# First norm tile by tile, gate projection of block 3 ahead of block 2's, and the GLU operand split between the last projection units

## The chip, the cores and the metric

The kernel runs on one core of a Trainium2 chip. The core has TensorE (PE, matmul), VectorE (DVE), ScalarE (ACT), GpSimd (POOL) and SyncE (SP, which here only issues transfers), each with its own in-order instruction stream, and 16 DMA engines. The metric is device microseconds of one execution, lower is better. The kernel before takes 2582.24 us, the median of 3 runs (2581.13 to 2583.32).

## The reference

Two residual layers with sandwich RMSNorm, for a prompt of 2048 tokens and 32 sample tokens that share the weights (model width 1024, float32):

```python
# layer 0, chunked gMLP
hn = rmsnorm(x, norm_pre[0])
u, v, z = split(hn @ w_in_a, 3)              # each 2048 wide
v = layernorm(v)
s = lower_triangular_mix_of_128(v) + b_s     # 8 groups
x = x + rmsnorm((u * s * silu(z)) @ w_out_a, norm_post[0])
# layer 1, S5
xb, z = split(rmsnorm(x, norm_pre[1]) @ w_in_b, 2)   # each 1024 wide
h = complex_diagonal_scan(xb)                # 64 groups of 16 channels, 64 states
y = gelu(Re(C h) + d_skip * xb)
y = (y @ w_glu1 + b_glu1) * sigmoid(y @ w_glu2 + b_glu2)
x = x + rmsnorm((y * silu(z)) @ w_out_b, norm_post[1])
```

It returns x for both groups, the normalised v rows of the sample and the last states.

## The kernel before

Every large product is float32 split in two float32r parts, high and low, and takes three matmuls (high by high, high by low, low by high; `mm3`, L62). The split of an operand is a cast on ScalarE (L69) and a subtraction on VectorE (L70). Weights come in pieces of 128x1024 (512 KB) through a staging tile `wst` and are split into `whi` and `wlo` (`weight`, L72).

The 2048 prompt tokens are four blocks of 512; the 32 sample tokens ride with block 3, so a product over block 3 that has tokens as its free dimension takes two banks of 256 and 288 columns, where another block takes one of 512 (`cols`, L317).

*Start.* `layer_a` (L478) loads four tiles x of 128 tokens, and for each: two squares on ScalarE (L135), the mean and a root by Newton steps on VectorE (L104 to L109, L136, L137), the product with the norm's gain (L140), eight PE transposes (L146) and the split into `hn`. Ahead of it 40 warm-up matmuls on a tile of ones run on PE (L193). Then `v_phase` (L250) multiplies `hn` with `wv`, weight piece by weight piece, over four banks (one for each tile of 128 tokens).

*End of layer B.* `layer_b` (L757) makes the inputs of the state space, the states `S` at every eighth position (a scan on VectorE), and then two things side by side: the last 16 pieces of the gate projection (`z_phase`, L846, one piece of 128 channels over one block each, first the 8 of block 2 and then the 8 of block 3) and 16 projection units (`s5_out`, L920). A unit loads T, Xo and Co (and, every second unit, Go) by SP, copies states into H on ScalarE, runs four matmuls with T and Xo and four with Co and H, takes the gelu on ScalarE into `Y` (L957), and stores `Y` to the DRAM tensor `yd` from GpSimd (L960). Each z piece is copied on ScalarE and stored from ScalarE's queue (L860; for block 3 the sample's columns too, L859).

*Start of layer C.* `layer_c` (L997) reads `yd` back, piece k of 128 channels at a time, into staging tiles `yst` (`load_y`, L1018) and splits it into `y`. One piece needs two units: k = 0 the units 0 and 2, k = 4 the units 1 and 3, and so on; the order of the pieces is `KO = (0, 4, 1, 5, 2, 6, 3, 7)`. `glu` (L1033) then multiplies `y` with two weights for each of 8 channel pieces.

The order in which instructions stand on each engine is set when the program is built, by a scheduler that takes the emitted order, the dependencies and its own model of times. On the chip each engine runs its stream in that order, and an instruction waits on semaphores for what it reads and for the buffer that it writes. Pools of buffers are stacked: a pool that opens after another has closed lies over its memory, and its first tile waits for the last use of the old one. So `y` (pool `yq`, opened after `hb3` has closed) lies over the normalised block 3.

Of the kernel before, what the change touches and what calls it, by code (L numbers as in the profile page):

```python
# [8 lines left out]
F32 = mybir.dt.float32  # L9
F32R = mybir.dt.float32r  # L10
# [9 lines left out]
TB = 512  # L20
NS = 32
TX = TB + NS
AL = 512
TXP = 640
# [6 lines left out]
KO = (0, 4, 1, 5, 2, 6, 3, 7)  # L31
# [3 lines left out]
class Trunk:  # L35
# [151 lines left out]
    def consts_a(self, c, tmp):  # L187
        nc, I = self.nc, self.I
        self.one = c.tile([128, 128], F32, name="one")
        nc.vector.memset(self.one, 1.0)  # L190

        b = self.aux()
        for i in range(40):  # L193
            self.mm(b[:, 0:128], self.one, self.one, True, True)
        self.gpre = self.load_gpre(c, 0)
        self.consts()
# [53 lines left out]
    def v_phase(self, b, hn, hook=None):  # L250
        nc, I = self.nc, self.I
# [7 lines left out]
        for n in range(4):  # L259
            bk = [self.bank() for _ in range(4 + smp)]  # L260
            for kp in range(4):
                w = self.weight(I["wv"][n, kp], (2, 512))
                for kk in range(2):
                    k = kp * 2 + kk
                    wk = (w[0][:, kk], w[1][:, kk])
                    f, l = k == 0, k == 7
                    for i in range(4):
                        c = slice(i * 128, i * 128 + 128)
                        self.mm3(bk[i], (hn[:, 0, k, c], hn[:, 1, k, c]), wk, f, l)
                    if smp:  # L270
                        self.mm_sample(bk[4][:64, :], self.stk[:, k], wk, f, l)
            vq = self.vg.tile([128, 4, 512], F32, tag="vg", name="vq", align_bytes=AL)
            for i in range(4):
                nc.scalar.copy(vq[:, i], bk[i])
                nc.vector.bn_stats(st[:, i, n], bk[i])
            self.vq.append(vq)
            if hook:
                hook(n)
            if smp:
                vs = self.vs[:NS, n * 512:n * 512 + 512]  # L280
                self.fold_sample(vs, bk[4])
                nc.vector.bn_stats(sts[:, n], vs)
# [195 lines left out]
    def layer_a(self):  # L478
        I = self.I
        with ExitStack() as s:  # L480
# [5 lines left out]
            xs0 = self.prep_load([I["xp"][0, 0]], 128)  # L486
            self.consts_a(ca, self.xp)
            hn, jobs = self.prep_jobs(0, I["xp"][0], I["xs"], self.gpre, self.hnp, "hn", None, 1)
            xs = [xs0] + [f() for f, _ in jobs[1:]]
            for (_, f), x in zip(jobs, xs):  # L490
                f(x)
            self.pin = True
            fin = None

# [11 lines left out]
            for b in range(NB):  # L506
# [6 lines left out]
                if b + 1 < NB:  # L513
# [3 lines left out]
                    hn, jobs = self.prep_jobs(b + 1, I["xp"][b + 1], I["xs"], self.gpre, self.hnp, "hn", self.stk)  # L517
                else:
                    g1 = self.load_gpre(ca, 1)
                    hn, jobs = self.prep_jobs(0, self.x1c(0), None, g1, self.hnp, "hn")  # L520
# [236 lines left out]
    def layer_b(self, s0):  # L757
        with ExitStack() as sr:
            zp = s0.enter_context(self.pool("zp", 2))
            with ExitStack() as s1:  # L760
                hb3 = s1.enter_context(self.pool("hb3"))
                with ExitStack() as s2:
                    hb2 = s2.enter_context(self.pool("hb2"))
                    with ExitStack() as s3:
                        hb1 = s3.enter_context(self.pool("hb1"))
                        with ExitStack() as s4:
# [5 lines left out]
                            jobs = []  # L772
# [13 lines left out]
                            for _ in steps:  # L786
                                pass
                        S = self.hnp.tile([128, 32, 2, CW + 1], F32, tag="hn", name="S",
                                          align_bytes=AL).rearrange("p g r c -> p r g c")
# [15 lines left out]
                    opa = sr.enter_context(self.pool("opa", 2, side="right"))  # L805
                    fp = sr.enter_context(self.pool("fp", side="right"))
                    out = self.s5_out(fp, opa, opb, S)
                    n = 0
                    for i in range(16):
                        if i == 8:  # L810
                            s2.close()
                        self.z_phase(zp, [2 + i // 8], [i % 8])
                        while n < 16 and n * 13 <= i * 15:
                            next(out)
                            n += 1
            self.yq = s0.enter_context(self.pool("yq"))
            self.yp = s0.enter_context(self.pool("yp", 2))
            self.y0 = self.load_y(0)

    def relay(self, dst, o, c0, n):  # L820

# [98 lines left out]
    def s5_out(self, fp, opa, opb, S):  # L920
        nc, I = self.nc, self.I
# [3 lines left out]
        for u in range(16):  # L925
            gl, gh, gu = (u // 2) * 4, u % 2, ((u // 2) % 2) * 4
            fb = u // 4 + 4 * gh
            g0 = fb * 8 + gu
            T = opa.tile([128, 4, 128], F32, tag="T", name="T", bufs=4)
            nc.sync.dma_start(T, self.td[fb][:, gu:gu + 4])  # L930
            X = opa.tile([128, 4, 2, CW], F32, tag="X", name="Xo", bufs=4)
            self.load_x(X, fb, gu, 4)
# [13 lines left out]
            p = slice(gh * 64, gh * 64 + 64)  # L946
# [50 lines left out]
    def layer_c(self):  # L997
        nc, I = self.nc, self.I
        with ExitStack() as s:
# [12 lines left out]
            for q in range(4):  # L1012
# [2 lines left out]
                    y = self.load_y(q + 1)  # L1015
                self.out_b(q, m, stk)

    def load_y(self, q):  # L1018
        nc = self.nc
        y = self.yq.tile([128, 2, 8, TXP], F32R, tag="y", name="y", align_bytes=AL)  # L1020
        for k in KO:
            t = self.yp.tile([128, TX], F32, tag="y", name="yst")
            n = TB
            nc.sync.dma_start(t[:, :TB].rearrange("p (j c) -> p j c", j=4),
                              self.yd[k].rearrange("j k g c -> (k g) j c")[:, 4 * q:4 * q + 4, :])
            if q == 3:
                n = TX
                nc.sync.dma_start(t[:, TB:].rearrange("p (j c) -> p j c", j=4),
                                  self.ysd[k].rearrange("j k g c -> (k g) j c"))
            self.split(y[:, 0, k, :n], y[:, 1, k, :n], t[:, :n])  # L1030
        return y

    def glu(self, q, y):  # L1033
# [212 lines left out]
```

## Time and profile before

| what | value |
|---|---|
| median of 3 runs | 2582.24 us (2581.13 to 2583.32) |
| the profiled execution | 2583.09 us |
| its span in the profile | 2581.3 us |
| PE busy | 2554.0 us, 99% |
| VectorE, ScalarE, GpSimd busy | 58%, 36%, 17% |
| mean rate of the DMA engines | 145 GB/s |

The span is the time from the first to the last instruction of the profiled execution; what is between it and that execution's own time, 1.8 us, lies around it. PE is the engine to read: its busy time is modelled from the issue of matmuls, so small gaps in it are best seen in the list of PE's waits and in the timeline, where a row has its start, its length, its engine, line and operands, and in brackets the idle time before it with what ended it. A view by windows gives the busy time of each engine in a stretch, the clock granted to PE (1.00 is full speed) and the share of the DMA engines.

### The profile page before, as it was taken

How to read it: one execution, taken by the hardware profiler on the slowest of the kernel's cores; microseconds unless marked ns; L12 is line 12 of the kernel's file. 1: busy time of each engine (PE TensorE's matmuls, PEld its weight loads, DVE VectorE, ACT ScalarE, POOL GpSimd, SP SyncE). 2: the span in 40 equal slices, each digit the busy share in tenths (PEclk: the TensorE clock that was granted, in tenths of full speed). 3: DMA queues.
4: the chain of work that ended last, by engine and by line, in shares of the span. 5: the costliest groups of instructions: out<-in, count | busy, mean ns of one | idle time of the engine just before them, and what ended most of it. 6: DMA issues, size and time to landing. Idle time of an engine off the chain costs nothing.

```text
span 2581.3 us, 34682 instructions
## 1 busy us (share of the span) xinstructions
PE 2554.0 (99%) x13163; PEld 2183.2 (85%) x13163; DVE 1501.7 (58%) x2809; ACT 926.2 (36%) x1520; POOL 429.5 (17%) x624
## 2 busy tenths in 40 slices
PE   9999999999999999999999999999999999999998
PEld 8888888788888888887999877889888888888896
DVE  5955657745655755744633547417897346464645
ACT  3322443323443222532222344325556433434331
POOL 0345100455100000000100120000023212121220
PEclk9999999999999999999999999999999999999999
DMA  5333424343534454343322346537699545454533
GB/s 168 100 127 112 135 95 151 116 122 115 153 116 130 163 162 155 109 138 93 105 78 82 107 128 191 145 110 212 215 321 303 186 132 183 138 183 144 163 123 102
DMA packets 220631, 375.04 MB, mean 145 GB/s; under 512 B 59520, under 2 KB 135808, under 8 KB 220464
## 3 DMA queue, kind: packets, MB, share of 16 engines
q1 hardware_dynamic: 165728, 308.09, 37.6%
q0 software_dynamic: 13600, 39.90, 4.9%
q10 hardware_dynamic: 41136, 24.84, 3.4%
q8 instruction: 103, 1.69, 0.3%
q14 instruction: 64, 0.52, 0.1%
HBM read 311.64 MB, written 61.11 MB: 144 GB/s over the span
## 4 chain that ended last, share of the span: by engine, by line
PE 89%; DVE 5%; DMA 3%; issue 1%; ACT 1%; SPq 0%; POOL 0%; DVEq 0%; ACTq 0%; POOLq 0%
PE mm L60 85%; PE aux L60 3%; DMA x<-in_xp_dram 1%; DVE wlo L70 1%; PE aux L146 1%; DMA x<-x1d 1%; ACT junk L135 0%; DMA T<-td 0%; DMA Xo<-xd 0%; DVE nt L107 0%; DMA wst<-in_wib_dram 0%; ACT whi L69 0%; DVE o L175 0%; DVE nt L108 0%; DMA Xi<-xd 0%
## 5 line engine op out<-in xcount | busy, mean ns | idle before, releaser
L60 PE MATMUL mm<-hn,whi 128*128 128x512 f32 (+2 forms) x3840 | 1011.1, 351 | 0.0
L70 DVE TENSOR_TENSOR wlo<-wst,whi 128x1024 fp32r<-128x1024 f32 x400 | 516.3, 1292 | 536.0 <-ACT whi L69 520.6
L60 PEld LDWEIGHTS mm<-hn,whi 128*128 128x128 f32 x3840 | 671.6, 189 | 88.0 <-DVE a L345 0.2
L69 ACT CAST whi<-wst 128x1024 fp32r<-128x1024 f32 x400 | 419.7, 1050 | 860.4 <-PE mm L60 758.6
L60 PE MATMUL mm<-hn,wlo 128*128 128x512 f32 (+2 forms) x1920 | 673.2, 351 | 2.9 <-DVE wlo L70 2.9
L60 PEld LDWEIGHTS mm<-hn,wlo 128*128 128x128 f32 x1920 | 361.7, 188 | 48.4 <-DVE wlo L70 3.3
L60 PE MATMUL mm<-y,whi 128*128 128x512 f32 (+2 forms) x1280 | 333.8, 350 | 3.1 <-ACT y L69 2.9
L60 PE MATMUL mm<-whi,gs 128*128 128x512 f32 x1024 | 328.4, 393 | 2.2 <-ACT a L344 1.4
L60 PE MATMUL mm<-whi,hn 128*128 128x512 f32 x1024 | 324.4, 392 | 0.6 <-ACT hn L69 0.6
L60 PEld LDWEIGHTS mm<-y,whi 128*128 128x128 f32 x1280 | 224.7, 188 | 34.8 <-ACT y L69 3.6
L60 PEld LDWEIGHTS mm<-whi,gs 128*128 128x128 f32 x1024 | 191.6, 188 | 44.9 <-ACT a L344 1.7
L60 PEld LDWEIGHTS mm<-whi,hn 128*128 128x128 f32 x1024 | 192.6, 189 | 43.5 <-ACT hn L69 0.9
L60 PE MATMUL mm<-y,wlo 128*128 128x512 f32 (+2 forms) x640 | 223.1, 349 | 0.0
L60 PE MATMUL mm<-wlo,hn 128*128 128x512 f32 x512 | 200.2, 391 | 0.1
L60 PE MATMUL mm<-wlo,gs 128*128 128x512 f32 x512 | 199.8, 390 | 0.0
L70 DVE TENSOR_TENSOR gs<-gq,gs 128x512 fp32r<-128x512 f32 (+1 forms) x128 | 91.1, 714 | 133.7 <-ACT gs L69 133.4
L60 PE MATMUL mm<-whi,m 128*128 128x512 f32 x512 | 159.8, 389 | 0.0
L69 ACT CAST gs<-gq 128x512 fp32r<-128x512 f32 (+1 forms) x128 | 80.5, 629 | 190.3 <-PE mm L60 175.4
L60 PEld LDWEIGHTS mm<-y,wlo 128*128 128x128 f32 x640 | 120.8, 189 | 15.1
L60 PEld LDWEIGHTS mm<-wlo,hn 128*128 128x128 f32 x512 | 96.4, 188 | 21.5 <-DVE wlo L70 0.5
L358 DVE SCALAR_TENSOR_TENSOR gq<-mm,lng,Rp 128x512 f32<-128x512 f32 x64 | 47.9, 748 | 114.5 <-PE mm L60 114.5
L60 PEld LDWEIGHTS mm<-whi,m 128*128 128x128 f32 x512 | 96.1, 188 | 20.7
(287 smaller groups left out, 2624.0 us busy)
## 6 DMA issues: line engine op xcount, KB each, us to landing
wst<-in_wuz_dram SPq DMA_DIRECT2D x128, 512.0 KB
wst<-in_wv_dram SPq DMA_DIRECT2D x64, 512.0 KB
wst<-in_woa_dram SPq DMA_DIRECT2D x64, 512.0 KB
wst<-in_wg_dram SPq DMA_DIRECT2D x64, 512.0 KB
wst<-in_wib_dram SPq DMA_DIRECT2D x48, 512.0 KB
wst<-in_wob_dram SPq DMA_DIRECT2D x32, 512.0 KB
Xi<-xd SPq DMA_DIRECT2D x32, 272.0 KB
Xo<-xd SPq DMA_DIRECT2D x32, 272.0 KB
```

Source lines behind the costliest of these rows:

```text
L60: self.nc.tensor.matmul(out, lhsT, rhs, start=start, stop=stop)
L69: self.nc.scalar.copy(hi, src)
L70: return (e or self.nc.vector).tensor_tensor(lo, src, hi.bitcast(F32), SUB)
L146: nc.tensor.transpose(b[:, k * 128:k * 128 + P], x[:, o:o + 128], self.ident[:P, :P])
L358: nc.vector.scalar_tensor_tensor(g3, s3, self.lng[:, db:db + 1], R, MUL, ADD)
```

## The change

1. The warm-up is 32 matmuls instead of 40.
2. The first norm goes tile by tile: each x tile is loaded and at once squared, rooted, scaled, transposed and split, and the first two `wv` pieces are loaded and split ahead of the tiles 1, 2 and 3 (kept in `self.pre`, from which `v_phase` takes them).
3. The last 16 gate projection pieces do block 3 first, then block 2.
4. The pool of block 3's normalised input, `hb3`, lives on as `self.yq`, and `y` for the first GLU block takes its tile, once block 3's pieces are emitted (i == 8). Six of `y`'s eight pieces are loaded and split one at a time behind the z pieces i = 9 to 14 (`y_part`), the last two after the loop. For this the staging tile comes from the pool `zp`, one buffer.
5. T has 3 buffers instead of 4, and `y` is 512 columns wide (544 for the last block) instead of 640.

```diff
-        for i in range(40):
+        for i in range(32):
             self.mm(b[:, 0:128], self.one, self.one, True, True)
...
-                w = self.weight(I["wv"][n, kp], (2, 512))
+                w = self.pre.pop(0) if self.pre else self.weight(I["wv"][n, kp], (2, 512))
...
-            xs = [xs0] + [f() for f, _ in jobs[1:]]
-            for (_, f), x in zip(jobs, xs):
-                f(x)
+            self.pre = []
+            for i, (load, rest) in enumerate(jobs):
+                if i < 2:
+                    self.pre.append(self.weight(I["wv"][0, i], (2, 512)))
+                rest(load() if i else xs0)
...
-                hb3 = s1.enter_context(self.pool("hb3"))
+                hb3 = self.yq = s0.enter_context(self.pool("hb3"))
...
                     for i in range(16):
+                        self.z_phase(zp, [3 - i // 8], [i % 8])
                         if i == 8:
-                            s2.close()
-                        self.z_phase(zp, [2 + i // 8], [i % 8])
+                            self.y0 = self.y_tile(0)
+                        if 9 <= i < 15:
+                            self.y_part(zp, self.y0, 0, KO[i - 9])
                         while n < 16 and n * 13 <= i * 15:
                             next(out)
                             n += 1
-            self.yq = s0.enter_context(self.pool("yq"))
+            for k in KO[6:]:
+                self.y_part(zp, self.y0, 0, k)
             self.yp = s0.enter_context(self.pool("yp", 2))
-            self.y0 = self.load_y(0)
...
-            T = opa.tile([128, 4, 128], F32, tag="T", name="T", bufs=4)
+            T = opa.tile([128, 4, 128], F32, tag="T", name="T", bufs=3)
...
+    def y_tile(self, q):
+        return self.yq.tile([128, 2, 8, TX if q == 3 else TB], F32R, tag="hb3", name="y", align_bytes=256)
+
+    def y_part(self, pool, y, q, k):
+
+        nc = self.nc
+        n = TX if q == 3 else TB
+        t = pool.tile([128, TX if q else TB], F32, tag="y", name="yst", bufs=2 if q else 1)
+        nc.sync.dma_start(t[:, :TB].rearrange("p (j c) -> p j c", j=4),
+                          self.yd[k].rearrange("j k g c -> (k g) j c")[:, 4 * q:4 * q + 4, :])
+        if q == 3:
+            nc.sync.dma_start(t[:, TB:].rearrange("p (j c) -> p j c", j=4),
+                              self.ysd[k].rearrange("j k g c -> (k g) j c"))
+        self.split(y[:, 0, k, :n], y[:, 1, k, :n], t[:, :n])
+
     def load_y(self, q):
-        nc = self.nc
-        y = self.yq.tile([128, 2, 8, TXP], F32R, tag="y", name="y", align_bytes=AL)
+        y = self.y_tile(q)
         for k in KO:
...
+            self.y_part(self.yp, y, q, k)
         return y
```

The line numbers of the changed kernel are 10 higher at the end of the file, 4 higher in the units (L961 is the gelu that was L957). The built orders of the two kernels differ in the start, in layer B's end, and in when one gain vector is loaded. Three places:

VectorE at the start, before: x0's root steps (L107 to L109) run through to the gain product of x0 (L140).

```order
L109 SCALAR_TENSOR_TENSOR rs<-nt,rs 128x1
L107 TENSOR_TENSOR nt<-rs 128x1
L108 SCALAR_TENSOR_TENSOR nt<-nt,ms 128x1
L109 SCALAR_TENSOR_TENSOR rs<-nt,rs 128x1
L136 TENSOR_TENSOR ms<-ss 128x1
L140 SCALAR_TENSOR_TENSOR x<-x,rs,gpre 128x1024
```

VectorE at the same place now:

```order
L108 SCALAR_TENSOR_TENSOR nt<-nt,ms 128x1
L70 TENSOR_TENSOR wlo<-wst,whi 128x1024
L109 SCALAR_TENSOR_TENSOR rs<-nt,rs 128x1
L140 SCALAR_TENSOR_TENSOR x<-x,rs,gpre 128x1024
L70 TENSOR_TENSOR wlo<-wst,whi 128x1024
L136 TENSOR_TENSOR ms<-ss 128x1
```

The low parts of the first two weight pieces now stand around x0's product and ahead of everything of x1; on PE, 13 matmuls on x0 stand between the transposes of x0 and those of x1, where there were 2.

ScalarE around unit 15 (the last), before: its gelus are the last of eight in a row, and the casts of `y` come later, behind all z copies.

```order
L957 ACTIVATE Y<-aux 128x264 x7
L1060 ACT_TABLE_LOAD
L1060 ACTIVATE gs<-zt 128x512 x2
L823 COPY z<-mm 128x2x16x8
L69 CAST whi<-wst 128x1024
...
L69 CAST whi<-wst 128x1024 x2
L823 COPY z<-mm 128x2x16x8
L858 COPY zs<-mm 128x32
L69 CAST y<-yst 128x512 x2
```

ScalarE there now (the first cast of `y` is piece k = 3, the second k = 7):

```order
L961 ACTIVATE Y<-aux 128x264 x5
L69 CAST y<-yst 128x512
L961 ACTIVATE Y<-aux 128x264 x2
L1070 ACT_TABLE_LOAD
L1070 ACTIVATE gs<-zt 128x512 x2
L69 CAST whi<-wst 128x1024
L827 COPY z<-mm 128x4x16x8
L864 DMA zd_115<-z 128x512
L69 CAST y<-yst 128x512
L69 CAST whi<-wst 128x1024 x2
```

Six casts of `y` stand earlier among the units; the seventh stands ahead of the last two gelus of unit 15, and the eighth ahead of the casts of two weights.

SP's loads around the middle units, before: the first two loads of `y` stand together, with the two bias vectors, ahead of unit 11's T and Xo (the Co there is unit 9's).

```order
L930 DMA T<-td_87 128x512
L934 DMA Co<-cod_79 128x512
L865 DMA Xo<-xd_103 128x4x136 x2
L1024 DMA yst<-yd_133 128x4x128
L1024 DMA yst<-yd_137 128x4x128
L1009 DMA bg_17579<-in_bg_dram 128x8
L1009 DMA bg_17581<-in_bg_dram 128x8
L930 DMA T<-td_91 128x512
```

SP's loads of `y` now, at its third and fourth pieces:

```order
L938 DMA Co<-cod_83 128x512
L1030 DMA yst<-yd_134 128x4x128
L869 DMA Xo<-xd_108 128x4x136 x2
L941 DMA Go<-gd_124 128x1024
L82 DMA wst<-in_wib_dram 128x1024
L934 DMA T<-td_92 128x512
L938 DMA Co<-cod_80 128x512
L1030 DMA yst<-yd_138 128x4x128
```

Each load of `y` now stands alone between the loads of units and weights, and the bias vectors come behind the last of them.

More of the change, by code (lines that the diff above doesn't have):

```diff
@@ L1016, in layer_c @@
                 self.out_b(q, m, stk)
+    def y_tile(self, q):
[10 more added lines that the diff above has]
+        self.split(y[:, 0, k, :n], y[:, 1, k, :n], t[:, :n])
     def load_y(self, q):
-        nc = self.nc
-        y = self.yq.tile([128, 2, 8, TXP], F32R, tag="y", name="y", align_bytes=AL)
+        y = self.y_tile(q)
         for k in KO:
[L1022 to L1030, printed above, removed]
+            self.y_part(self.yp, y, q, k)
         return y
```

## The prediction

> **What bounds the kernel now.** I read the page's sums and chain first, then PE's waits, then windows around each wait.
>
> ```profile
> PE 2554.0 (99%) x13163; PEld 2183.2 (85%) x13163; DVE 1501.7 (58%) x2809; ACT 926.2 (36%) x1520; POOL 429.5 (17%) x624
> PE 89%; DVE 5%; DMA 3%; issue 1%; ACT 1%; SPq 0%; POOL 0%; DVEq 0%; ACTq 0%; POOLq 0%
> ...
> PE mm L60 <- ACT y L69: 2.9, 1, 2.9
> PE mm L60 <- DVE wlo L70: 2.9, 1, 2.9
> PE aux L60 <- ACT Y L957: 2.8, 2, 2.2
> PE aux L146 <- DVE hn L70: 1.4, 1, 1.4
> ```
>
> TensorE is busy for 2554.0 of 2581.3 us, and the change takes no matmul away except eight warm-ups. So it can win only what PE loses, and it touches three of the places: the first transposes (L146), the gelus `Y` of the projection units (L957), and the first GLU piece `y` (L69). The wait on `wlo` lies near 1580 us, in layer B's projections, and stays.
>
> Idle time isn't all that PE loses there:
>
> ```profile
> 6.83:13.66 6.83, 6.83 (x63) 6.80 (x62) 5.17 (x37) 5.09 (x13) 0.00 (x0) 1.00 0.80 326
> 13.66:17.07 3.41, 1.20 (x4) 0.37 (x2) 3.41 (x10) 2.20 (x4) 0.00 (x0) 1.00 0.29 83
> 17.07:20.49 3.42, 3.40 (x10) 2.90 (x11) 3.42 (x5) 1.53 (x2) 0.00 (x0) 0.50 0.56 184
> ...
> 1949.02:1952.43 3.41, 1.20 (x5) 1.06 (x6) 3.34 (x7) 1.62 (x5) 0.11 (x1) 1.00 1.15 326
> 1952.43:1955.84 3.41, 3.41 (x9) 2.67 (x8) 3.41 (x14) 2.74 (x7) 2.02 (x3) 0.50 1.01 323
> 2027.53:2030.94 3.41, 0.85 (x4) 0.67 (x4) 2.79 (x3) 3.03 (x6) 0.00 (x0) 1.00 0.43 98
> 2030.94:2034.35 3.41, 3.41 (x10) 2.50 (x9) 0.78 (x2) 0.00 (x0) 0.00 (x0) 0.50 0.92 340
> ```
>
> In these rows stand the stretch, its length, PE's busy time, four more engines, the granted clock (third from the end), the DMA share and GB/s. Three times a stretch of 3.41 us in which PE was busy for 1.2, 1.2 and 0.85 us is followed by one at clock 0.50. Half clock for 3.41 us costs 1.7 us of work. So each of the three places loses its idle time and 1.7 us more.
>
> **Part A, the start.** Warm-ups fall from 40 to 32, and the first two `wv` weights are loaded and split ahead of x1 to x3.
>
> ```profile
> 12.83 1.04 PE L146 MATMUL aux<-ident,x 128*128 128x128 f32 x8
> 14.51 0.50 PE L60 MATMUL mm<-whi,hn 128*128 128x512 f32 x1 [0.64 <-ACT hn L69]
> 17.09 1.12 PE L146 MATMUL aux<-ident,x 128*128 128x128 f32 x4 [1.43 <-DVE hn L70]
> ...
> 10.05 1.28 DVE L140 SCALAR_TENSOR_TENSOR x<-x,rs,gpre 128x1024 f32<-128x1024 f32 x1
> 13.88 1.23 DVE L70 TENSOR_TENSOR wlo<-wst,whi 128x1024 fp32r<-128x1024 f32 x1
> 15.02 1.28 DVE L140 SCALAR_TENSOR_TENSOR x<-x,rs,gpre 128x1024 f32<-128x1024 f32 x1
> 18.40 1.04 ACT L69 CAST whi<-wst 128x1024 fp32r<-128x1024 f32 x1 [2.51 <-DMA wst<-in_wv_dram]
> ```
>
> PE loses 0.64 + 1.43 us idle and 1.7 us at half clock, 3.8 us in all. In the new order VectorE splits the first weight (1.23 us) before the last step of x0's root, so x0's product (L140) starts about 0.8 us later, at 10.85, and its transposes at 12.2 instead of 12.83; that they are earlier at all is because fewer warm-ups stand ahead of them. Then 13 matmuls run on x0 alone, where 2 ran. But x1's product comes behind the second weight's split, two `hn` splits and the root steps of x1 and x2: summing those durations I get about 18.0 instead of 15.02, so PE stands again for some 1.5 to 2 us before x1's transposes. The idle time is shifted, hardly reduced. Whether a half-clock stretch follows hangs on the stretch up to 17.07 or up to 20.49, in which I find PE about a third busy, just where the rows above begin to be followed by one. The first bank group then ends 0.8 us earlier without such a stretch and 0.7 us later with it. I take 0; bounds -0.8 and +0.7.
>
> **Part B, the units among the gate projection.**
>
> ```profile
> 1898.91 2.02 PE L60 MATMUL aux<-H,Co 128*128 128x264 f32 x8 [0.53 <-issue]
> 1905.84 0.71 PE L60 MATMUL aux<-Xo,T 128*128 128x264 f32 x2 [0.58 <-ACT Y L957]
> 1909.06 0.61 PE L60 MATMUL aux<-H,Co 128*128 128x264 f32 x2
> 1947.84 0.40 PE L60 MATMUL mm<-hn,whi 128*128 128x256 f32 x2
> 1948.60 0.40 PE L60 MATMUL mm<-hn,whi 128*128 128x256 f32 x2
> 1951.23 1.87 PE L60 MATMUL aux<-Xo,T 128*128 128x264 f32 x6 [2.23 <-ACT Y L957]
> ...
> 1947.45 0.58 ACT L823 COPY z<-mm 128x512 f32<-128x512 f32 x1
> 1950.29 0.33 ACTq L860 DMA_DIRECT2D zd<-z  x1
> 1950.79 1.24 ACT L957 ACTIVATE Y<-aux 128x264 f32<-128x264 f32 x4 [2.76 <-DMA T<-td]
> ...
> 1941.06 1.74 SPq L930 DMA_DIRECT2D T<-td  x1
> ...
> 1896.91 2.54 ACT L950 COPY H<-Go 64x512 f32<-64x512 f32 x4 [3.29 <-DMA Xo<-xd]
> ...
> 1880.00:1960.00 80.00, 76.66 (x351) 64.15 (x351) 76.14 (x190) 50.59 (x97) 23.16 (x36) 0.98 1.00 335
> ```
>
> Here PE loses 0.53, 0.58 and 2.23 us idle and one half-clock stretch, 5.0 us. The ACT rows tell how the longest comes about: ScalarE copied z by 1948.0, but could issue z's store only at 1950.29, when the T load issued at 1941.06 (unit 10's) had landed, nine microseconds later under a full DMA (share 1.00 over the 80 us); the four gelus of unit 7 stood behind that store, and unit 8 had no free bank. Unit 0's 0.53 us come in the same way: its H copies started at 1896.91, behind a z store that an `Xo` load held.
>
> With block 3 first, eight projections of 48 matmuls of 256 or 288 columns come in this stretch instead of 24 of 512. Six such matmuls take 0.76 us (1947.84 to 1948.60), so 48 take 6.1 us. The 24 of block 2 take 5.5 to 5.7 us by the same rate per column. Up to unit 8 eight projections run, so the units there get some 4 us more time for the same loads, and unit 0's loads start 5.8 us earlier: in the SP order they now stand behind an earlier weight. The first `y` loads no longer stand in a pair, with the two `bg` loads, in front of unit 11's loads.
>
> Against it: units 0 to 3 now come closer together. VectorE makes their states in pairs:
>
> ```profile
> 1906.09 1.65 DVE L943 SCALAR_TENSOR_TENSOR Go<-S,d,Go 128x128 f32<-128x128 f32 x6
> ```
>
> Units 2 and 3's states are ready at 1907.7 before, and H after two more copies. In the new VectorE order two weight splits (1.15 us each) no longer stand ahead of them, so 1905.4 and H at 1906.7, against a need at about 1906.8. Unit 0's states are ready at 1894.8 as before, so its H, 2.1 us of copies later, at 1896.9, against a need at about 1896.6. The `Co` buffers have as little slack. I leave 0.9 us there (bounds 0 and 5) and nothing at unit 8, where both the states and the loads have 3 to 4 us to spare. T with 3 buffers instead of 4 lets a load wait for the unit three back: that is still over 9 us ahead of its use from unit 4 on. Sum of B: 0.9 - 5.0 = -4.1 us, bounds -5.0 and 0.
>
> **Part C, the start of the GLU.**
>
> ```profile
> 2029.07 0.36 ACT L823 COPY z<-mm 128x256 f32<-128x256 f32 x1
> 2029.41 0.63 ACT L69 CAST y<-yst 128x512 fp32r<-128x512 f32 x1
> 2030.09 1.87 PE L60 MATMUL mm<-y,whi 128*128 128x512 f32 x5 [2.93 <-ACT y L69]
> ...
> yd<-Y POOLq DMA_DIRECT2D x32, 256.0 KB, 6.2
> ...
> 2031.14 12.28 SPq L1024 DMA_DIRECT2D yst<-yd  x6
> 2036.66 1.37 ACT L69 CAST y<-yst 128x512 fp32r<-128x512 f32 x2 [6.10 <-DMA yst<-yd]
> 2040.89 0.62 ACT L69 CAST y<-yst 128x512 fp32r<-128x512 f32 x1 [2.86 <-DMA yst<-yd]
> ```
>
> Before, `y`'s buffer lies over hb3, which the last z matmul still reads, so the first cast waits for it: 2.93 us idle and 1.7 at half clock, 4.6 us. The later pieces are late too, but are covered, because four banks use each piece in turn. Now six pieces are split during units 7 to 13, on engines with room (ACT is 36% busy), and cost nothing. The last two can't be: piece k=3 needs units 12 and 14, piece k=7 units 13 and 15. On ScalarE the cast of k=3 stands between the second and third gelu of unit 15, so unit 15's store waits for the load of k=3.
>
> Count from P, PE's end of unit 14: gelus 0.8, GpSimd's issue 0.3, store 6.2, load of k=3 2.9 (what ACT waited for at 2040.89), cast 0.6, two gelus 0.7, issue 0.3, store 6.2, load of k=7 2.9, cast 0.6: P + 21.5. PE meanwhile has 11 z matmuls (2.6), unit 15 (3.6, as 1905.84 to 1909.5), 13 more (3.1), the final transposes (0.4), the last 24 (5.7) and 21 matmuls on seven pieces (5.0): P + 20.4. It then waits about 1.2 us, in a stretch busy enough to keep the clock. With both loads at 5.5 us (2031.14 to 2036.66) the wait is 6.3 us and a half-clock stretch follows; with stores 1 us faster there is none. Behind k=7's cast on ScalarE stands the cast of the next GLU weight, needed some 3 us later. Sum of C: 1.2 - 4.6 = -3.4, bounds -4.6 and +3.
>
> **The sum.** The profiled execution took 2583.09 us; the sum is 2583.1 + 0 - 4.1 - 3.4 = 2575.6. It lies 0.85 us over the median of the runs shown, a third of my smallest term, so I predict 2575.5 without a correction.
>
> **Rivals.**
> (1) *The GLU wait only moves*: k=7 is as late as the first piece was, 2.9 us and a half-clock stretch. For it: two stores and two loads in series, ScalarE blocked in between. Against: DMA is less than full there (0.43 and 0.92 in the windows). 2583.1 - 4.1 = 2579.0.
> (2) *The units' stalls stay*: VectorE and DMA are both full from 1880 to 1960, and the block order changes neither's work. For it: 76.14 of 80 us and share 1.00 in the row above. Against: 4 us more time per eight units. 2583.1 - 3.4 - 0.5 = 2579.2.
> (3) *No half-clock stretch after waits this short at the start*, so A gives its -0.8: 2574.8. The Trainium skill, "TensorE: Matmul & The Clock Gate", section "HAM oscillation — how this bites in real kernels", gives as its rule "no PE-idle gaps >~3.4µs"; by it gaps of 2.23 and 2.93 us would have cost no clock, and the rows show that they did.
> (4) *Slower*: stores of z on ScalarE. Block 3 has two of them for each projection (z and the sample's), 16 issues in the full stretch where there were 8, and each can wait for some load as the one at 1950.29 did, with gelus behind it. One in eight cost 2.2 + 1.7 = 3.9 us. If four of the 16 did so, 15.7 - 5.0 - 3.4 = +7.3: 2590.4. It decides from three on (+3.3). Against it: the loads that they would wait for are issued earlier than before, by my count 8 us or more ahead.
> That the split pieces are not early after all is covered by (1): only the last two pieces set the start.
>
> **How the numbers follow.** Forecast 0.55, (1) 0.17, (2) 0.13, (3) 0.05, (4) 0.07, the rest unnamed. The forecast's own range is 2571.5 to 2578.5 (all three terms at their good bounds give -10.4). To hold 8 in 10 it must take in (1) and (2) with their spread: 2570.5 to 2582.5. A measurement of this kernel can tell 0.2%, 5.2 us, from no change: faster is under 2577.1, slower over 2587.4. The forecast lies mostly below the first bound, (3) too, (1) and (2) mostly above it: faster 0.60, same 0.33, slower 0.07.
>
> **What would show it.** Right: no PE wait above 1 us on `Y` between 1880 and 1960 and clock 1.00 there; the first GLU matmul right behind the last z matmul, 24 matmuls on one bank, and a wait of about 1 us before its last three on a cast of `y`; at the start 13 matmuls between x0's and x1's transposes, and the 97th v matmul within 1 us of before's. Wrong: a wait of over 3 us on k=7 with clock 0.50 behind it, a z store on ScalarE with gelus waiting behind it, or a wait on VectorE's states at units 0 to 3.

## The result, and the profile after

The changed kernel takes 2568.07 us (median of 4 runs, 2566.77 to 2569.72) against 2581.99 us for the kernel before (4 runs beside it, 2581.13 to 2583.32): a ratio of 0.9946, 95% interval 0.9931 to 0.9961. That is 13.9 us faster. The forecast was 2575.5, so the gain is about twice the forecast one, and the time lies 2.4 us under the low end of the range. Its profiled execution took 2568.73 us.

The page of the changed kernel, its sums and its chain, and then TensorE's waits (engine and line, what was waited for, us in total, times, longest):

```profile
PE 2545.2 (99%) x13147; PEld 2176.5 (85%) x13147; DVE 1497.0 (58%) x2809; ACT 926.0 (36%) x1520; POOL 439.1 (17%) x624
PE 95%; DVE 2%; DMA 1%; issue 1%; ACT 0%; POOL 0%; SPq 0%; DVEq 0%; ACTq 0%; POOLq 0%
...
PE mm L60 <- DVE wlo L70: 2.9, 1, 2.9
PE mm L60 <- DVE vq L315: 2.6, 3, 1.8
PE aux L146 <- DVE x L140: 1.5, 1, 1.5
PE aux L146 <- DVE hn L70: 1.3, 2, 0.7
```

TensorE's share of the chain rose from 89% to 95%. The waits on `y` and `Y` are gone altogether, not just smaller. A wait in layer A, at which no edit is aimed, is gone too: 1.4 us on `a` (L344). New is a wait of 1.5 us on `x` (L140), at the start.

Windows over the start before, and then over the start, the end of layer B and the start of the GLU after:

```profile
0.00:50.00 50.00, 46.72 (x240) 40.22 (x241) 28.90 (x83) 20.73 (x36) 0.67 (x5) 0.97 0.51 167
...
0.00:50.00 50.00, 45.72 (x234) 37.95 (x235) 29.95 (x89) 21.71 (x37) 0.67 (x5) 1.00 0.52 182
1880.00:1960.00 80.00, 80.00 (x486) 73.27 (x485) 78.09 (x190) 57.17 (x120) 35.51 (x40) 1.00 1.03 343
2000.00:2050.00 50.00, 50.00 (x225) 41.48 (x224) 18.81 (x19) 19.27 (x30) 10.72 (x12) 1.00 0.63 201
```

From 1880 to 1960 TensorE is now busy for 80.00 of 80 us (76.66 before), although VectorE and the DMA are fuller than they were: 78.09 us and a share of 1.03. In all three stretches the granted clock is 1.00; each of them held a stretch at 0.50 before. In the first 50 us TensorE stands idle for longer than before, 4.3 us against 3.3.

Where the 14.5 us between the two spans arise can be read from the same instruction in both traces. The first gate activation of layer A, a group of transposes near 1620 us and a gate product in the first GLU block, before:

```profile
123.63 0.60 ACT L344 ACTIVATE a<-mm 128x512 f32<-128x512 f32 x1
...
1622.78 1.91 PE L146 MATMUL aux<-ident,x 128*128 128x128 f32 x16
...
2099.88 0.74 DVE L1057 SCALAR_TENSOR_TENSOR ga<-mm,bg,ga 128x512 f32<-128x512 f32 x1
```

and after:

```profile
121.24 0.60 ACT L344 ACTIVATE a<-mm 128x512 f32<-128x512 f32 x1
...
1618.83 1.91 PE L146 MATMUL aux<-ident,x 128*128 128x128 f32 x16
...
2084.58 0.75 DVE L1067 SCALAR_TENSOR_TENSOR ga<-mm,bg,ga 128x512 f32<-128x512 f32 x1
```

So 2.4 us come from the start, another 1.6 us (net) from places in between that the change does not edit, and 11.3 us from layer B's end and the start of the GLU. That makes 15.3; 0.8 us of it is lost again in the last GLU block. The second profile of the changed kernel (below) loses only 0.1 us there, so that loss belongs to the execution.

### The profile page after: what moved, and what is told of

It reads as the page before. It is cut to its first block, busy times and chain, and to the rows that moved or that the text cites. A ratio compares the mean times of both kernels' runs of the same rounds, so it can differ in the third digit from the quotient of the medians.

```text
span 2566.8 us, 34660 instructions
## 1 busy us (share of the span) xinstructions
PE 2545.2 (99%) x13147; PEld 2176.5 (85%) x13147; DVE 1497.0 (58%) x2809; ACT 926.0 (36%) x1520; POOL 439.1 (17%) x624
## 4 chain that ended last, share of the span: by engine, by line
PE 95%; DVE 2%; DMA 1%; issue 1%; ACT 0%; POOL 0%; SPq 0%; DVEq 0%; ACTq 0%; POOLq 0%
PE mm L60 90%; PE aux L60 4%; PE aux L146 1%; DMA x<-in_xp_dram 1%; DVE wlo L70 0%; DVE nt L107 0%; ACT junk L135 0%; DMA wst<-in_wib_dram 0%; DVE xr L176 0%; DVE x L140 0%; DVE nt L108 0%; DMA crs<-in_crs_dram 0%; DVE ms L114 0%; DVE rs L109 0%; DVE hn L70 0%
```

## The experiments

All were timed against the kernel before. The times are medians, and the intervals are those of the ratio.

### The two halves apart

The start alone (32 warm-ups, two weights ahead, tile by tile):

```diff
-        for i in range(40):
+        for i in range(32):
...
-                w = self.weight(I["wv"][n, kp], (2, 512))
+                w = self.pre.pop(0) if self.pre else self.weight(I["wv"][n, kp], (2, 512))
...
+            for i, (load, rest) in enumerate(jobs):
+                if i < 2:
+                    self.pre.append(self.weight(I["wv"][0, i], (2, 512)))
+                rest(load() if i else xs0)
```

> The start alone (32 warm-ups, first norm tile by tile, two weights ahead), layer B and C as before. Theory (the parts add up, each by the loss it removes): in the trace of the change the first weights' matmuls run 2.4 us ahead and stay so, so 2.4 us faster than before, about 2579.6, with the waits of 0.5, 0.6, 2.2 and 2.9 us in layer B's end unchanged. Rival (as the prediction had it, the start gives nothing): 2582.0, within 1 us. A half-clock stretch more or less moves either by 1.7 us.

Measured: 2577.83 us against 2581.43, ratio 0.9987 (0.9978 to 0.9996): 3.6 us faster. Its trace keeps the waits of layer B's end and of the GLU. Its first gate activation comes at 121.61, 2.0 us earlier than before; the rest of the 3.6 arises later, or is within the interval (1.0 to 5.7 us).

The other half alone, that is the block order, `y` in block 3's buffer piece by piece, and 3 buffers for T, with the start as before:

```diff
-                hb3 = s1.enter_context(self.pool("hb3"))
+                hb3 = self.yq = s0.enter_context(self.pool("hb3"))
...
+                        self.z_phase(zp, [3 - i // 8], [i % 8])
                         if i == 8:
-                            s2.close()
-                        self.z_phase(zp, [2 + i // 8], [i % 8])
+                            self.y0 = self.y_tile(0)
+                        if 9 <= i < 15:
+                            self.y_part(zp, self.y0, 0, KO[i - 9])
...
-            T = opa.tile([128, 4, 128], F32, tag="T", name="T", bufs=4)
+            T = opa.tile([128, 4, 128], F32, tag="T", name="T", bufs=3)
```

> The end of layer B alone (block 3 first, y in its buffer and split piece by piece, T with 3 buffers), the start as before. Theory: the whole loss there goes, 11.3 us by the trace of the change, so about 2570.7, and the profile shows no wait above 0.3 us between 1880 and 2050. Rival (the sizes of the prediction): 7.5 us, 2574.5, with a wait of about 1 us on the last piece of y.

Measured: 2572.69 us against 2581.43, ratio 0.9964 (0.9952 to 0.9977): 8.7 us faster. No wait on `Y` or `y` is left; the one of 0.5 us before unit 0's first H matmul is. Together the halves give 12.3 us, which agrees with the whole within the intervals. The start, costed at nothing, gives 2 to 4 us of it.

### What the start's gain hangs on

Tile by tile with 32 warm-ups, but no weights ahead (the edit is against the start alone), and the reverse: 32 warm-ups and two weights ahead, with the four tiles loaded together as before (the line that this adds to the kernel before).

```diff
-                if i < 2:
+                if i < 0:
                     self.pre.append(self.weight(I["wv"][0, i], (2, 512)))
```

> The start with 32 warm-ups and the norm tile by tile, but no weights ahead of the tiles; the rest as before. Theory (the gain of the start, 3.6 us with all of it, comes from the weights ahead: PE has matmuls on x0 right behind its transposes, and the half-clock stretch at 17 us goes): no gain, 2581.4 within 1 us, and a half-clock stretch near 17 us. Rival (it is the tile-by-tile order or the fewer warm-ups): 2577.8, as with the whole start.

```diff
             hn, jobs = self.prep_jobs(0, I["xp"][0], I["xs"], self.gpre, self.hnp, "hn", None, 1)
+            self.pre = [self.weight(I["wv"][0, i], (2, 512)) for i in range(2)]
             xs = [xs0] + [f() for f, _ in jobs[1:]]
```

> The start with 32 warm-ups and the two weights ahead of the tiles 1 to 3, but all tiles loaded and then normed as before. Theory (the weights ahead are the gain): 2577.8, as with the whole start, and no half-clock stretch near 17 us. Rival (the tile-by-tile order is): 2581.4.

Measured: tile by tile alone 2581.19 us, ratio 0.9998 (0.9990 to 1.0007), so nothing; weights ahead alone 2579.68, ratio 0.9990 (0.9981 to 0.9999), some 2.6 us by the ratio. The kernel with the tiles alone waits for the weight's high part, and half clock follows. A row of its waits, and two of its windows:

```profile
PE mm L60 <- ACT whi L69: 2.5, 1, 2.5
...
11.59:15.00 3.41, 0.90 (x8) 0.65 (x6) 3.05 (x22) 3.35 (x8) 0.00 (x0) 1.00 0.21 84
15.00:18.42 3.42, 2.77 (x7) 1.84 (x7) 3.42 (x7) 0.70 (x1) 0.00 (x0) 0.50 0.40 135
```

So the start's gain is the early weights, and it is clock and not idle time. None of the nine profiles with the weights ahead (the change, its repetitions and variants, and both starts) shows half clock in the first 25 us; all five without them do. In the nine the first gate activation comes between 121.2 and 121.8 us, in the five between 123.2 and 124.0.

The eight warm-ups put back into the change (40 for 32):

> The change with 40 warm-ups instead of 32. Theory (PE waits 1.5 us behind the warm-ups for x0's product, so eight more of 0.11 us hide in it): the same as the change, 13 us under before, 2568 to 2569. Rival (the warm-ups stand on the path): 0.9 us more than the change, or 2.6 if a half-clock stretch comes with it, 2569 to 2571.

Measured: 2571.54 us, ratio 0.9964 (0.9951 to 0.9976). The interval overlaps that of the change, and part of its difference lies elsewhere: in its profile unit 0 waits 1.7 us behind a z store, and the wait near 1572 us is followed by half clock. Each warm-up is two matmuls in the trace (80 rows for 40), so eight of them take some 1.8 us, twice what the expectation had; the change's wait of 1.5 us for x0's product hides most of it. The first gate activation comes at 121.83, 0.6 us later than in the change, so little of the difference in time is the warm-ups' own.

### The block order alone, and the z stores alone

The prediction put TensorE's waits on `Y` down to a z store on ScalarE that waits for a load, with the gelus behind it. Two experiments take these waits away without touching `y`. First, block 3 ahead of block 2, with everything else as before:

```diff
-                        if i == 8:
-                            s2.close()
-                        self.z_phase(zp, [2 + i // 8], [i % 8])
+                        self.z_phase(zp, [3 - i // 8], [i % 8])
```

> Only the block order of the last 16 gate projection pieces is changed (block 3 first), T has 4 buffers, y is loaded as before. Theory (the order alone clears the units' stalls, by more PE time for the same loads): the waits between 1880 and 1960 go and the first GLU wait of 2.9 us stays: 5 to 6 us faster, 2576 to 2577. Rival (it is the early loads of y or the buffers of T that clear them): the waits stay, 2582 within 1 us.

Second, the kernel before with the z stores of these two blocks issued from GpSimd:

```diff
-                        nc.scalar.dma_start(self.zsd[fb], zs)
-                nc.scalar.dma_start(self.zd[fb][:, b], z)
+                        nc.gpsimd.dma_start(self.zsd[fb], zs)
+                (nc.gpsimd if b > 1 else nc.scalar).dma_start(self.zd[fb][:, b], z)
```

> The kernel before with one change: the z stores of blocks 2 and 3 are issued from GpSimd instead of ScalarE. Theory (a z store that must wait for a load holds ScalarE and the gelus behind it): the wait of 2.2 us before unit 8 goes, and with it its half-clock stretch, 2.2 to 4 us faster, 2578 to 2580, though GpSimd's stores of Y may now be held in the same way. Rival (the units wait for their loads or for VectorE's states, whoever stores z): the waits stay, 2582 within 1 us.

Measured: the order alone 2582.66 us, ratio 1.0004 (0.9996 to 1.0013); the stores alone 2581.53, ratio 0.9999 (0.9990 to 1.0008). Both are nothing. Yet both did what they should to the units. With the order alone the waits of 0.58 and 2.23 us on `Y` are gone; with the stores moved, no gelu stands behind a z store any more. The time came back out in the next place. The first row is of the waits with the order alone; behind it stand two windows at the start of its GLU, then rows of SP, ScalarE and TensorE there:

```profile
PE mm L60 <- ACT y L69: 6.3, 1, 6.3
...
2028.16:2031.57 3.41, 1.52 (x4) 1.23 (x5) 2.18 (x3) 1.24 (x2) 0.00 (x0) 0.50 1.06 311
2031.57:2034.99 3.42, 3.42 (x10) 2.65 (x9) 0.00 (x0) 0.00 (x0) 0.00 (x0) 0.50 1.04 386
...
2023.77 1.09 SPq L1022 DMA_DIRECT2D yst<-yd  x2
2029.38 0.62 ACT L69 CAST y<-yst 128x512 fp32r<-128x512 f32 x1 [1.39 <-DMA yst<-yd]
2030.05 2.50 PE L60 MATMUL mm<-y,whi 128*128 128x512 f32 x5 [6.31 <-ACT y L69]
```

The units finished earlier and the last z matmul with them, but the first `y` load is issued only at 2023.77, when that matmul has ended, because the first `y` is staged over block 2's buffer. Then come a load, a cast, and the wait of 6.31 us, with two stretches at half clock where before there was one. The order alone also has a wait of 2.7 us at unit 0, behind a z store. In the kernel with the z stores moved the same happens with `Co` and `y`:

```profile
PE mm L60 <- ACT y L69: 4.7, 1, 4.7
PE aux L60 <- DMA Co<-cod: 2.1, 2, 1.3
...
2020.19 0.33 SPq L82 DMA_DIRECT2D wst<-in_wg_dram  x1
2025.11 1.04 ACT L69 CAST whi<-wst 128x1024 fp32r<-128x1024 f32 x1 [6.26 <-DMA wst<-in_wg_dram]
```

Here the weight's load is issued at 2020.19 and the cast of `y` stands behind the cast of that weight. So the cause named in the prediction for the waits on `Y` holds, and yet taking the waits away is worth nothing by itself: what comes next is set by other things and doesn't come earlier.

### What the GLU's start hangs on

All eight pieces of `y` written behind the units in the code, through the same single staging buffer:

```diff
-                        if 9 <= i < 15:
-                            self.y_part(zp, self.y0, 0, KO[i - 9])
...
-            for k in KO[6:]:
+            for k in KO:
                 self.y_part(zp, self.y0, 0, k)
```

> The change with all eight pieces of y split after the units, through the same single staging buffer (none of them among units 9 to 14). Theory (the early pieces carry the GLU's part of the gain: what was won among the units is kept only if y is ready when the last z matmul ends): in the change one piece takes a load of 2.7 to 3.1 us, a cast of 0.62 and a subtraction of 0.69, so 4 to 4.5 us a piece when one staging buffer takes them in turn, 33 to 36 us for eight; the first load can go at about 1993, behind unit 15's loads, so the last piece is there at about 2027 against a need at 2021.8 in the change. PE waits 5 to 8 us on a cast of y near 2017 to 2022, half clock behind it for one or two pieces of 3.41 us: 6 to 10 us over the change, 2574 to 2578. Rival (the order and the buffer's place carry it, the pieces are hidden anyway): no wait on y over 1 us, 2568 as the change.

Measured: 2568.15 us, ratio 0.9944 (0.9930 to 0.9957), the same as the change. The theory fell, and its premise with it: where the lines stand in the code hardly matters here. In the trace of this kernel the second to sixth loads of `y` and their casts still run among the units (the sixth cast):

```profile
1992.43 0.61 ACT L69 CAST y<-yst 128x512 fp32r<-128x512 f32 x1
```

The change has these loads from 1949.88 to 1989.78, and the sixth cast at 1993.13: the same within 4 us for each. The instructions of an engine are put in order after the code is written, and by this run a piece goes in when its buffers are free. So the next run takes the freedom away instead of the place in the code: `y` stays in block 3's buffer, but its first pieces are staged in the GLU's own two buffers, which lie over block 2's.

```diff
-                        if 9 <= i < 15:
-                            self.y_part(zp, self.y0, 0, KO[i - 9])
...
-            for k in KO[6:]:
-                self.y_part(zp, self.y0, 0, k)
             self.yp = s0.enter_context(self.pool("yp", 2))
+            for k in KO:
+                self.y_part(self.yp, self.y0, 0, k)
...
-        t = pool.tile([128, TX if q else TB], F32, tag="y", name="yst", bufs=2 if q else 1)
+        t = pool.tile([128, TX if q else TB], F32, tag="y", name="yst", bufs=2)
```

> The change with one thing undone: the first y is staged in the GLU's own staging buffers (two of them, which lie over block 2's hn) instead of in the projections' pool; y itself stays in block 3's buffer. Theory (the gain at the GLU comes from staging that is free before the last z matmul): the first load can go only when the last z matmul has read block 2's buffer, 2017 in the change; it takes 2.7 to 5.5 us, the cast 0.62, so PE waits 3.5 to 6.5 us on a cast of y and then runs a stretch or two of 3.41 us at half clock, as with the order alone (6.31 us there): 6 to 10 us over the change, 2574 to 2578. Rival (the buffer that y itself lies in is what counts, and the loads find their place anyway): no wait on y over 1 us, 2568.

Measured: 2578.66 us, ratio 0.9987 (0.9978 to 0.9996): some 10 us over the change, though its units run without a loss (80.00 of 80 us). Its longest wait, the stretch of the GLU's start, the first two loads and the first cast:

```profile
PE mm L60 <- ACT y L69: 6.7, 1, 6.7
...
2000.00:2050.00 50.00, 43.29 (x187) 35.43 (x186) 16.69 (x20) 19.75 (x30) 9.47 (x11) 0.93 0.62 188
...
2016.14 1.11 SPq L1028 DMA_DIRECT2D yst<-yd  x2
2022.14 0.62 ACT L69 CAST y<-yst 128x512 fp32r<-128x512 f32 x1 [1.05 <-DMA yst<-yd]
```

It is the picture of the order alone again: the load waits for the last z matmul, and the wait on `y` is 6.7 us. In these runs the time won among the units is kept only where the first `y` has a staging buffer that is free before the last z matmul ends. What such a buffer would give without the new block order was not run.

### The change again, and two variants of it

> The change once more, beside the next run. Both theories: 2568 to 2570, 12 to 14 us under before. Its profile tells which of its waits are the same each time: the start (no half-clock stretch by 25 us) and the GLU start (no wait) by my theory; unit 0's H (0 to 2 us) and the half clock after the wait near 1573 us may differ.

Measured: 2567.05 us (2565.95 to 2572.35) against 2582.85, ratio 0.9942 (0.9929 to 0.9956). The result stands, with the same waits.

The change with the z stores of both blocks issued from GpSimd, as in the run above:

> The change, with the z stores of blocks 2 and 3 issued from GpSimd instead of ScalarE. Theory (z stores held by loads are what is left of the units' waits, on H of unit 0): that wait is gone in its profile, and as y is no longer behind the weights' casts at the GLU start nothing takes the time back: 0 to 2 us faster than the change. Rival (held z stores on GpSimd now hold the stores of Y, and the last pieces of y come late): a wait at the GLU start, 2 us or more slower than the change.

Measured: 2570.37 us, ratio 0.9953 (0.9939 to 0.9967), not faster than the change. What the z stores still cost there is too little to be seen.

The wait on `wlo` near 1572 us, the longest that is left, stands beside the residual adds of layer A's last block. The change with block 3's adds and stores moved to GpSimd:

```diff
-                                 [I["xp"][b, i] for i in range(4)], [x1[i] for i in range(4)], 1 if smp else 2)
+                                 [I["xp"][b, i] for i in range(4)], [x1[i] for i in range(4)], 0 if smp else 2)
```

> The change, and block 3's last residual adds in layer A (four of 128x1024, 1.2 us each on VectorE) and their stores go to GpSimd. Theory (the wait of 2.9 us near 1573 us is a weight's low part queued behind four products and two of these adds on VectorE): it shrinks by about 2.3 us, 1 to 4 us faster than the change with the half-clock stretch that sometimes follows, 2564 to 2567. Rival (GpSimd's adds slow VectorE beside them, as one small VectorE instruction took 2.36 us beside a GpSimd add there): the wait stays or grows, 2568 to 2571.

Measured: 2578.72 us, ratio 0.9986 (0.9977 to 0.9994), some 10 us slower than the change. Its wait and two windows there:

```profile
PE mm L60 <- DVE wlo L70: 7.0, 1, 7.0
...
1573.70:1577.13 3.43, 0.00 (x0) 0.00 (x0) 3.43 (x2) 0.00 (x0) 3.41 (x3) 1.00 0.37 74
1577.13:1580.54 3.41, 1.16 (x2) 0.50 (x2) 3.41 (x17) 0.00 (x0) 1.46 (x2) 0.50 0.61 157
```

The wait grew from 2.9 to 7.0 us, and half clock followed. In the first window VectorE is busy for the whole 3.43 us with two instructions, while GpSimd adds; the four products ahead of the weight's low part took 9.08 us there and 4.86 in the change. No variant beat the change.

## Why the prediction was right and wrong

**What bounds the kernel: right.** TensorE is busy 99% of the time, the change could win only what TensorE lost, and idle time costs more where half clock follows.

**Part A, taken as 0 (bounds -0.8 and +0.7): wrong.** It measured -3.6 us alone, of which -2.0 by the activation's row, and -2.4 by that row in the change. The step that failed is that x1's product would come at "about 18.0 instead of 15.02", so that TensorE "stands again for some 1.5 to 2 us". In the profile after:

```profile
11.56 1.09 PE L146 MATMUL aux<-ident,x 128*128 128x128 f32 x8 [1.50 <-DVE x L140]
...
10.22 1.28 DVE L140 SCALAR_TENSOR_TENSOR x<-x,rs,gpre 128x1024 f32<-128x1024 f32 x1
16.40 1.28 DVE L140 SCALAR_TENSOR_TENSOR x<-x,rs,gpre 128x1024 f32<-128x1024 f32 x1
17.82 1.06 PE L146 MATMUL aux<-ident,x 128*128 128x128 f32 x8 [0.37 <-DVE nt L108]
```

x0's product starts at 10.22, where I had 10.85 for it, and x1's at 16.40: 6.2 us pass between them, where I had 7.15. I had added up the rows of the root steps, but those of x1 and of x2 overlap in time. TensorE stands for 0.27 us on `whi` and 0.37 us before x1's transposes. Nor is x1's product decisive: with 40 warm-ups it starts at 18.15, as late as I had it, and TensorE stands for only 0.05 us before x1's transposes, with 18 matmuls on x0 ahead of them in the order built for that kernel. In the change TensorE is busy for 3.15 and 2.93 us of the windows that follow:

```profile
13.65:17.07 3.42, 3.15 (x13) 1.96 (x12) 3.42 (x23) 3.18 (x8) 0.00 (x0) 1.00 0.44 151
17.07:20.48 3.41, 2.93 (x15) 2.16 (x16) 3.38 (x11) 1.08 (x2) 0.00 (x0) 1.00 0.17 26
```

The prediction had TensorE "about a third busy" there. So the 1.7 us of half clock were won, and the wait before x1's transposes, but not idle time as a whole: 1.50 us of new wait, for x0's product, stand behind the shorter warm-up, as the first row above shows. My bounds held only idle time against one stretch, and left out that the second wait could vanish with its stretch.

**Part B, -4.1 us (bounds -5.0 and 0): right in its cause, a little small.** All of the 5.0 us that it listed went. It left 0.9 us on VectorE's states and `Co` for units 0 to 3. In the profile after nothing is left; the half alone still has 0.5 us there, and with 40 warm-ups it was 1.7 us. The term is the size of this scatter. But its sum assumes that what is won stays won. The order alone shows that without part C it would be 0, not -4.1: the parts aren't independent.

**Part C, -3.4 us (bounds -4.6 and +3): cause right, the stores costed too long.** All of the 4.6 us that it listed went. It counted two stores of 6.2 us in series, the median of all 32. The stores around unit 15, in the stretch from 2001 to 2020 (after), and the casts that end the two loads:

```profile
yd<-Y POOLq DMA_DIRECT2D x4, 256.0 KB, 3.7
...
2002.89 1.50 POOL L964 DMA_DIRECT2D yd<-Y  x2 [6.16 <-ACT Y L961]
2007.02 0.37 SPq L1030 DMA_DIRECT2D yst<-yd  x1
2009.78 0.62 ACT L69 CAST y<-yst 128x512 fp32r<-128x512 f32 x1 [2.89 <-DMA yst<-yd]
2011.26 1.50 POOL L964 DMA_DIRECT2D yd<-Y  x2 [6.25 <-ACT Y L961]
2014.08 0.38 SPq L1030 DMA_DIRECT2D yst<-yd  x1
2017.24 0.62 ACT L69 CAST y<-yst 128x512 fp32r<-128x512 f32 x1 [2.39 <-DMA yst<-yd]
2017.05 0.61 PE L60 MATMUL mm<-y,whi 128*128 128x512 f32 x2
```

From the first store's issue to the load behind it pass 4.1 us, and 2.8 us the second time; the median in this stretch is 3.7. With two stores of 6.2 the prediction put k = 7's cast at P + 20.9 to P + 21.5. P, the end of unit 14, is about 2002, so the cast ran at P + 15.2 to P + 15.9. The first GLU matmul starts at 2017.05 and needs k = 7 after 21 more at 0.227 us, at about 2021.8, which is P + 19.8 against the P + 20.4 forecast. The work of TensorE was counted right; the stores were not, and so k = 7 has 3 to 4 us to spare instead of being 1.2 us late. That ScalarE holds unit 15's last two gelus for the load of k = 3 did happen, as the rows show: the cast at 2009.78 waited 2.89 us and stood ahead of the gelus at 2010.30.

**The rest.** By the rows of the two spans A is -2.4 us, and B and C together -11.3. B and C had listed 9.6 us in all, so 1.7 us more were won there; they are in no row of TensorE's waits, and where they arise stays open. The 1.6 us between the start and layer B's end are in no term either. At 1450 us ScalarE's squares wait for a load of x, and TensorE behind them for `a`:

```profile
1450.14 0.63 ACT L135 ACTIVATE junk<-x 128x512 bf16<-128x512 f32 x1 [4.92 <-DMA x<-x1d]
```

is the row before, and after it is

```profile
1445.60 0.63 ACT L135 ACTIVATE junk<-x 128x512 bf16<-128x512 f32 x1 [2.98 <-DMA x<-x1d]
```

The load ended 4.5 us earlier where TensorE's own work was only 2.2 to 2.6 us earlier, and 1.4 us of wait went. This goes with the new start: in the eight profiles with both the weights ahead and the tiles one by one the wait on `a` is 0 to 0.6 us, in the six others (one of them with the weights ahead alone) 1.1 to 2.0. How the start does it isn't settled.

The stretch of half clock behind the wait near 1576 us, which the profile before has and the one after has not, is no source of gain. Transposes behind it, before and after:

```profile
1594.94 1.91 PE L146 MATMUL aux<-ident,x 128*128 128x128 f32 x16
...
1590.44 2.45 PE L146 MATMUL aux<-ident,x 128*128 128x128 f32 x16 [0.73 <-DVE hn L70]
```

Ahead of that wait TensorE is 4.1 us earlier than before, at the transposes that start at 1582.19 (1587.96 before) 5.8, at these 4.5, and from 1600 on 3.9 again: it then waits for VectorE and its transposes take longer (2.45 us against 1.91), and the time is taken back.

**The rivals.** (1), the wait on k = 7 as late as the first piece was: not seen. (2), the units' stalls stay since VectorE and DMA are full: not seen; both became fuller and TensorE lost nothing. (4), z stores on ScalarE holding the gelus: one such wait of 1.7 us with 40 warm-ups, and one of 2.7 us with the order alone, always at unit 0 and never four. (3), no half clock at the start: this is what happened, with a larger gain than its -0.8, because TensorE hardly stood before x1's transposes. It is not that waits this short cost no clock: in the profile before, they did. The place where the runs do bear a version of (1) is a kernel without the early staging.

## What to carry to other kernels

A wait that is taken away in a place where the next one is set by something else is worth nothing by itself: before crediting it, ask what the next stage waits for, and whether that starts earlier too (here the block order alone and the moved stores alone gave 0, and the block order with a staging buffer that is free early gave 8.7 us). Where the order of the instructions is made after the code is written, look at the buffers before the places of lines: here they decided what ran early. Where a load or a store is costed, take its time from rows of the same kind of stretch, not from the median over the kernel.

## What the runs showed of the hardware that was not expected

The clock changes only on a grid of 3.41 us, and the grid begins at another point in each execution: the first full-speed piece starts between 4.05 and 7.00 us in the fourteen profiles. In the one after it starts at 4.43, and half clock begins at 492.54 and 2561.01, which are 143 and 749 steps of 3.4133 us later. Whether a wait costs clock hangs on where it falls on the grid. The wait of 2.9 us on `wlo` near 1572 to 1576 us is the same in nearly all of them, and the windows on the grid read, before:

```profile
1576.97:1580.38 3.41, 0.54 (x2) 0.49 (x3) 3.41 (x4) 1.12 (x2) 0.00 (x0) 1.00 0.74 222
1580.38:1583.80 3.42, 3.42 (x9) 2.63 (x8) 3.42 (x11) 0.41 (x1) 0.00 (x0) 0.50 1.00 316
```

and after:

```profile
1571.15:1574.56 3.41, 1.64 (x8) 1.02 (x6) 3.41 (x6) 0.00 (x0) 0.00 (x0) 1.00 0.46 154
1574.56:1577.98 3.42, 2.29 (x10) 1.90 (x11) 3.42 (x6) 1.53 (x2) 0.00 (x0) 1.00 0.98 286
```

Before, the wait falls into one window (0.54 us busy, 16%), and half clock follows. After, it is spread over two (1.64 us and 2.29 us), and none does. Over the thirteen profiles with a wait of that length there, half clock followed in seven, where the emptiest window was up to 40% busy, and not in six, where it was 44% busy or more. Elsewhere it also followed windows up to 61% busy, so no sharp bound is shown. The Trainium skill, "TensorE: Matmul & The Clock Gate", section "Part 1: The HAM clock gate (the "warmup" mystery)", says that the window is 3413 ns and free-running; these rows agree. Its rule in "HAM oscillation — how this bites in real kernels", no idle gaps over some 3.4 us, would let a 2.9 us wait cost no clock; here half clock followed it in seven profiles of thirteen. So a wait of 2 to 3 us brought half clock, 1.7 us of work, by the chance of where it fell on the grid, which the prediction had treated as certain for the three places that it named. The kernel with the weights ahead alone shows it at one of them: it waits 2.9 us on `y` at the GLU's start, and the granted clock is 1.00 from 2000 to 2050. Nor need a stretch without half clock win time in the end: behind the wait near 1572 us the change had lost that lead again by 1600.
